# Queries and keys transposed and split in the projection stage and stored, in place of at each head pair of the attention

## The chip, the cores and the metric

One core of one Trainium2 chip runs the kernel. The metric is the device time of one execution in microseconds (us). The engines are TensorE (PE; its weight loads are shown as PEld), VectorE (DVE), ScalarE (ACT), GpSimd (POOL) and SyncE (SP). SP does no arithmetic in this kernel: it issues transfers. ACT and POOL issue transfers too, each in its own instruction stream. Every engine runs its instructions in the order in which they stand in its stream and waits at an instruction until what it needs is there.

## The reference

One inference step of a decoder layer for a prompt of 1024 rows (width 1024) and for 8 sample rows, which share all weights. Cut to what the change touches:

```python
h = rmsnorm(x) @ w_in                      # columns: q 512, k 512, v 512, gate logits 8, u 512, z 512
logf = log_sigmoid(h[..., O_F:O_U] + b_f)  # one forget gate per head and row
c = cumsum(logf, axis=1)
s = einsum('bqhd,bkhd->bhqk', q, k) * 64 ** -0.5      # 8 heads of 64
s = s + (c[query] - c[key])                            # causal mask behind it
att = einsum('bhqk,bkhd->bqhd', softmax(s), v)
```

Beside it the sample rows attend over 8192 cached keys each, in a paged cache (keys gathered, multiplied by the sample's query, summed over 64 columns). Then come a spatial gating of u and z, an output projection, a cross-attention into 256 memory rows and a gated MLP. The keys k and values v of the prompt are outputs too.

## The kernel before

**Three products for one.** All matrix products of the prompt run in a rounded 32-bit format with two parts: a number is split into a high part h (ACT copies it in the rounded format) and a low part l (DVE subtracts h from the number). A product is then three matmuls, h·h, h·l and l·h. The helper `split` (L232) does one split; weights arrive as `wr` and are split into `wh` (L235, ACT) and `wl` (L236, DVE).

**Stages of the prompt.** The projection, called p1, runs in column groups: Q, F (the 8 gate columns and u together, 520 columns), K, V, Z. A group loads four weight tiles of 128x1024 or 128x1040 and goes over eight row tiles of 128 rows, 24 matmuls each (F: 48 of 260 columns). `evac` (L467) then copies the bank with a row scale to a tile `t` and stores it: Q to the scratch `q_d`, K and V to the outputs. After p1 come the attentions of the first and of the second 512 rows, one behind the other; the first is mixed with the projection of the memory rows. Then come merge, cross-attention and MLP for the first and for the second half.

**Attention of one half** (`attention`, from L725). It goes over four head pairs, in each over blocks of queries and keys. The score product folds the split and the gates into the contraction: the operand `qq` has 64 rows of the query's high part over 64 rows of its low part, and a second piece with the high part and 4 gate rows; `ka` holds the key's high part twice, `kb` its low part with 4 gate rows. `load` (L730) loads a pair's queries and keys in rows, and the values. `setup` (L743) then transposes them on PE (L750 queries, L779 keys, four each), copies the high parts on ACT (L757, L784), copies these once more on POOL (L758, L785) and subtracts for the low parts on DVE (L774, L788). In the first half it also stores the split keys to `ks_d` from POOL (L791, L792), so that the second half loads those keys ready made. `LD` and `ST` are the places in the block loop at which the next pair's load and set-up are begun.

**The sample's work** is cut into steps that are mixed into the prompt's stages at a fixed pace (`PACE`, L76). In p1 a step gathers cached keys into `kv` (POOL), multiplies them by the sample's query `d` (DVE, L1444) and sums (DVE, L1448). That query is computed in group Q, stored by SP into `qs_d` (L465), and loaded from there spread over 128 partitions into `d` (SP, L1398).

**What sets the order.** The program is written as generators; a scheduler with a timeline model then puts each engine's instructions in order when the kernel is built. `behind(engine)` (L1369) and `issue_after` keep an instruction behind another one. The order is fixed before the run.

Of the kernel before, what the change touches and what calls it, by code (L numbers as in the profile page):

```python
# [60 lines left out]
LD = [(0, 1, 0), (0, 0, 0)]  # L61
ST = [(0, 1, 1), (0, 1, 1)]
# [5 lines left out]
NT = 7  # L68
# [3 lines left out]
SB = 2  # L72
# [6 lines left out]
def build(nc, tc, ctx, a, phases=None):  # L79
# [123 lines left out]
    q_d = dram.tile([T, AW], F32, tag="q_d", name="q_d")  # L203
# [6 lines left out]
    ks_d = dram.tile([NH, 64, 2, 512], F32, tag="ks_d", name="ks_d")  # L210
# [163 lines left out]
    def p1(early):  # L374
# [92 lines left out]
        def evac(ps, dst, sc, tt):  # L467
            t = T2()
            nc.scalar.activation(t, ps, AF.Copy, scale=sc[:, tt : tt + 1])
            nc.scalar.dma_start(dst[tt * P : (tt + 1) * P, :], t)  # L470
# [78 lines left out]
        for c0, dst in ((O_K, k_d), (O_V, v_d)):  # L549
            ws, sps = loaded(c0, 512, [(0, 512)])  # L550
            for tt in range(8):
                ps = BK()
                mm_chunk(tt, ws, ps, 0, 512)
                if tt == SD - 1:
# [15 lines left out]
                evac(ps, dst, rstd, tt)  # L570
# [155 lines left out]
    def attention(hf, queue, late=None, at=3):  # L726
# [3 lines left out]
        def load(hp):  # L730
            cs = slice(hp * P, (hp + 1) * P)
            qn = tpool.tile([P, 512], F32, tag="qn", bufs=1, name=nm("qn")).rearrange("p (i c) -> p i c", c=P)
            nc.sync.dma_start(qn, q_d[hf * 512 : (hf + 1) * 512, cs].rearrange("(i p) c -> p i c", p=P))
            if hf == 0:
                kvn = U([P, 2 * nk, P])
                kn, vn = kvn[:, :nk, :], kvn[:, nk:, :]
            else:
                kn, vn = T2().rearrange("p (i c) -> p i c", c=P), U([P, nk, P])
            nc.sync.dma_start(kn, k_d[hf * 512 : nk * P, cs].rearrange("(i p) c -> p i c", p=P))
            nc.sync.dma_start(vn, v_d[: nk * P, cs].rearrange("(i p) c -> p i c", p=P))  # L740
            return qn, kn, vn

        def setup(hp, qn, kn, vn):  # L743


            calm = lambda: tc.issue_after(lastexp[0]) if lastexp else nullcontext()
            with behind(ENG.PE):
                tr = BB() if hf else (MS, BB, BA)[SB]()
                for i in range(4):
                    nc.tensor.transpose(tr[:, i * P : (i + 1) * P], qn[:, i, :], ident)  # L750
            qab, ka, kb = [], [], []
            for j in range(2):
                h = hp * 2 + j
                rows = slice(64 * j, 64 * j + 64)
                qq = U([P, 2, 512], F32R)
                with calm():
                    nc.scalar.activation(qq[0:64, 0, :], tr[rows, :], AF.Copy)  # L757
                nc.gpsimd.tensor_copy(qq[0:64, 1, :], qq[0:64, 0, :].bitcast(F32))  # L758
                nc.gpsimd.dma_start(qq[64:68, 1, :], cq_d[h, :, hf * 512 : (hf + 1) * 512])
# [5 lines left out]
                else:  # L765
                    ka.append(U([P, nk * P], F32R))
                    kb.append(U([P, nk * P], F32R))
                    for r in range(2):
                        nc.sync.dma_start(ka[j][64 * r : 64 * r + 64, 0:512].bitcast(F32), ks_d[h, :, 0, :])
                    nc.sync.dma_start(kb[j][0:64, 0:512].bitcast(F32), ks_d[h, :, 1, :])  # L770
                nc.gpsimd.dma_start(kb[j][64:68, :], ck_d[h, :, : nk * P])
            for j, qq in enumerate(qab):
                rows = slice(64 * j, 64 * j + 64)
                nc.vector.tensor_tensor(qq[64:128, 0, :], tr[rows, :], qq[0:64, 0, :].bitcast(F32), op=ALU.subtract)  # L774
            yield
            with behind(ENG.PE):
                tr = BB() if hf else (MS, BB, BA)[SB]()
                for i in range(4):
                    nc.tensor.transpose(tr[:, i * P : (i + 1) * P], kn[:, i, :], ident)  # L779
# [110 lines left out]
        for _ in first:  # L890
            pass
# [1143 lines left out]
```

## Time and profile before

| | us |
|---|---|
| median of 3 runs | 1792.91 |
| lowest and highest run | 1789.93, 1795.33 |
| the profiled execution, first to last instruction | 1791.7 |
| PE busy | 1735.9 |
| DVE busy | 1399.9 |
| ACT busy | 733.5 |
| POOL busy | 488.3 |

The profile is one execution on its own; its span is what it has of a time of its own. A row of a time line reads: start, duration, engine (a q behind the name is its queue side, which issues transfers), line, operation, output <- inputs, shape, and in brackets the idle time ahead of it with what ended it. Names of tiles stand without their numbers there. PE's rows show 0.39 us for a matmul of 512 columns while the next begins 0.23 us later, since matmuls overlap. Group Q runs to 57.4 us, F from 62.2 to 111.8 us, Z ends at 239.95 us, the first scores of the attention start at 263.0 us and its last at 471.0 us.

### The profile page before, as it was taken

To read this page: it belongs to the slowest core of one execution; us is meant where nothing else is said; L and a number is where in the kernel's file an instruction comes from. 1 tells how busy PE (TensorE), PEld (TensorE's weight loads), DVE (VectorE), ACT (ScalarE), POOL (GpSimd) and SP (SyncE) were. 2 spreads that over 40 slices of the span, in tenths; PEclk is the share of its full clock that TensorE was granted. 3 is DMA by queue.
4 is the path that set the end of the run, shared out by engine and by line. 5 is a ranking of instruction groups with operands and counts; after the bars stand their busy time and mean duration, and the time that the engine had idled before them with its cause. 6 is when DMAs were issued, how large, how long until landed. Compare 5 with 4: busy or idle time off the path is not lost.

```text
span 1791.7 us, 25124 instructions
## 1 busy us (share of the span) xinstructions
PE 1735.9 (97%) x9653; PEld 1285.7 (72%) x9653; DVE 1399.9 (78%) x1733; ACT 733.5 (41%) x1374; POOL 488.3 (27%) x461
## 2 busy tenths in 40 slices
PE   8999999889999999999999999999999999999997
PEld 5787777655677666767777777766666778768875
DVE  4689658989788986989999999898885549855344
ACT  6332355566643635333333244335353233333232
POOL 1252234443222332333322223433322112102110
PEclk9999999999999999999999999999999999999999
DMA  8786798777697975779788788988879587568982
GB/s 291 297 304 226 294 334 319 259 264 244 254 403 279 363 299 224 282 285 345 290 301 313 291 317 311 376 306 346 320 280 350 214 306 249 191 260 297 359 310 80
DMA packets 157074, 521.06 MB, mean 291 GB/s; under 512 B 20874, under 2 KB 40842, under 8 KB 124186
## 3 DMA queue, kind: packets, MB, share of 16 engines
q0 software_dynamic: 57168, 341.14, 50.0%
q1 hardware_dynamic: 92874, 165.73, 26.5%
q10 hardware_dynamic: 6912, 12.59, 1.9%
q8 instruction: 76, 1.25, 0.3%
q14 instruction: 44, 0.36, 0.1%
HBM read 495.47 MB, written 23.93 MB: 290 GB/s over the span
## 4 chain that ended last, share of the span: by engine, by line
PE 53%; issue 9%; DMA 8%; DVE 6%; ACT 2%; POOL 2%; POOLq 0%; DVEq 0%; ACTq 0%; SPq 0%
DMA kv<-cache_v,io 6%; PE ba L272 6%; PE ba L274 6%; PE ba L273 6%; PE dv L1495 4%; PE bb L272 3%; PE bb L273 3%; PE bb L274 3%; PE ba L1063 1%; DVE s L1448 1%; PE ba L1064 1%; PE ba L1065 1%; PE dv L331 1%; DMA kv<-cache_k,io 1%; PE dv L1774 1%
## 5 line engine op out<-in xcount | busy, mean ns | idle before, releaser
L235 ACT ACTIVATE wh<-wr 128x1024 fp32r<-128x1024 f32 (+2 forms) x220 | 228.6, 1044 | 443.3 <-PE ba L273 142.3
L236 DVE TENSOR_TENSOR wl<-wr,wh 128x1024 fp32r<-128x1024 f32 (+2 forms) x220 | 262.7, 1200 | 165.1 <-PE ba L274 57.4
L1428 POOL DMA_INDIRECT kv<-cache_k,io x128 | 186.9, 1460 | 606.8 <-DVE s L1448 327.2
L1444 DVE TENSOR_TENSOR kv<-kv,d 128x1024 f32<-128x1024 f32 (+1 forms) x156 | 258.0, 1681 | 32.6 <-DMA kv<-cache_k,io 32.6
L1448 DVE TENSOR_REDUCE s<-kv 128x16 f32<-128x1024 f32 (+1 forms) x156 | 258.4, 1672 | 0.0
L1489 POOL DMA_INDIRECT kv<-cache_v,io x128 | 160.8, 1256 | 239.4 <-PE dv L1495 155.2
L272 PE MATMUL ba<-u,wh 128*128 128x512 f32 x528 | 209.3, 397 | 0.0
L274 PE MATMUL ba<-u,wl 128*128 128x512 f32 x528 | 209.0, 396 | 0.0
L273 PE MATMUL ba<-u,wh 128*128 128x512 f32 x528 | 208.5, 395 | 0.5 <-DVE u L239 0.5
L272 PE MATMUL ba<-wh,u 128*128 128x512 f32 (+1 forms) x495 | 186.1, 379 | 0.9 <-ACT u L235 0.9
L273 PE MATMUL ba<-wl,u 128*128 128x512 f32 (+1 forms) x495 | 185.1, 375 | 1.3 <-DVE wl L236 1.3
L274 PE MATMUL ba<-wh,u 128*128 128x512 f32 (+1 forms) x495 | 183.4, 375 | 0.0
L1495 PE MATMUL dv<-kv,s 128*32 128x512 f32 x1024 | 127.1, 598 | 1.6 <-DMA kv<-cache_v,io 1.6
L274 PEld LDWEIGHTS ba<-u,wl 128*128 128x128 f32 x528 | 99.2, 188 | 29.0 <-issue 6.5
L272 PEld LDWEIGHTS ba<-u,wh 128*128 128x128 f32 x528 | 99.3, 188 | 26.4 <-issue 4.8
L273 PEld LDWEIGHTS ba<-u,wh 128*128 128x128 f32 x528 | 99.2, 188 | 25.2 <-issue 2.3
L272 PEld LDWEIGHTS ba<-wh,u 128*128 128x128 f32 x495 | 93.0, 188 | 25.0 <-issue 6.5
L272 PE MATMUL bb<-u,wh 128*128 128x512 f32 x272 | 108.7, 400 | 0.0
L274 PE MATMUL bb<-u,wl 128*128 128x512 f32 x272 | 108.0, 398 | 0.0
L273 PE MATMUL bb<-u,wh 128*128 128x512 f32 x272 | 107.9, 397 | 0.0
L273 PEld LDWEIGHTS ba<-wl,u 128*128 128x128 f32 x495 | 93.0, 188 | 20.1 <-DVE wl L236 1.9
L274 PEld LDWEIGHTS ba<-wh,u 128*128 128x128 f32 x495 | 92.9, 188 | 19.5 <-issue 1.6
(454 smaller groups left out, 3310.6 us busy)
## 6 DMA issues: line engine op xcount, KB each, us to landing
wr<-w_up SPq DMA_DIRECT2D x88, 512.0 KB
kv<-w_up POOLq DMA_DIRECT2D x22, 1024.0 KB
wr<-w_down SPq DMA_DIRECT2D x40, 512.0 KB
kv<-w_down POOLq DMA_DIRECT2D x11, 1024.0 KB
wr<-w_in SPq DMA_DIRECT2D x16, 512.0 KB
wr<-w_o SPq DMA_DIRECT2D x16, 512.0 KB
wr<-w_cq SPq DMA_DIRECT2D x16, 512.0 KB
wr<-w_co SPq DMA_DIRECT2D x16, 512.0 KB
```

The lines of the kernel that those rows point to most:

```text
L235: nc.scalar.activation(h, src, AF.Copy)
L236: nc.vector.tensor_tensor(l, src, h.bitcast(F32), op=ALU.subtract)
L272: mmul(out, sh, mh, start=(i == 0), stop=False)
L273: mmul(out, sh, ml, start=False, stop=False)
L274: mmul(out, sl, mh, start=False, stop=(i == n - 1))
L331: mmul(ps[32 * j : 32 * j + 32, :w], xT[:, k, :] if nk == 8 else xT[:, k * 8 : k * 8 + 32], raw[:, q, j * w : (j + 1) * w], start=(k == 0) ...
L1063: mmul(pss[i], mh[k][:, tb], wh, start=(k == korder[0]), stop=False)
L1428: nc.gpsimd.indirect_dma_start(kv, None, a["cache_k"], off(kidx[:, b, ch : ch + 1]))
L1444: nc.vector.tensor_tensor(kvv[:, i : i + m, :], kvv[:, i : i + m, :], qb.unsqueeze(1).broadcast_to((P, m, 512)), op=ALU.mult)
L1448: nc.vector.tensor_reduce(s[:, ch * 4 + i : ch * 4 + i + m, :].rearrange("p k h -> p (k h)"), kvv[:, i : i + m, :].rearrange("p k (h d) -> ...
L1489: nc.gpsimd.indirect_dma_start(kv, None, a["cache_v"], off(kidx[:, b, ch : ch + 1]))
L1495: mmul(dv[32 * j : 32 * j + 32, :], s[:, ch * 4 : ch * 4 + 4, :].rearrange("p k h -> p (k h)"), kvv[:, j, :], start=(ch == 1), stop=(ch == ...
```

## The change

Queries and keys are now transposed and split behind the projection's tiles, by a new function `operand`: it transposes the evacuated tile (four transposes into one bank), splits the bank into h and l (128x512, two heads' 64 columns at once per transpose), and stores both into two new scratch tensors, `qt_d` and `kt_d`, which hold for each head 64 rows of high and 64 rows of low part over all 1024 positions. The two stores of h are issued by ACT, the two of l by SP, 64 rows of 4x128 columns each. An `operand` is not run with its tile but put on a list; `turn_over` runs the oldest one or two behind a later tile's matmuls. `q_d` and `ks_d` are gone, and K and V are still stored by `evac`.

In the attentions `load` now loads `qq`, `ka` and `kb` ready made, eleven loads per head pair from SP, and `setup` is gone with its transposes, copies, casts, subtractions, stores and yields. The second half loads a pair at place (0, 1, 0) of the block loop in place of (0, 0, 0). The pool of 512-column tiles has 8 buffers in place of 7, for which the one `qn` buffer is gone.

```diff
-LD = [(0, 1, 0), (0, 0, 0)]
-ST = [(0, 1, 1), (0, 1, 1)]
+LD = [(0, 1, 0), (0, 1, 0)]
-NT = 7
+NT = 8
-    q_d = dram.tile([T, AW], F32, tag="q_d", name="q_d")
+    qt_d = dram.tile([NH, P, T], F32, tag="qt_d", name="qt_d")
+    kt_d = dram.tile([NH, P, T], F32, tag="kt_d", name="kt_d")
-    ks_d = dram.tile([NH, 64, 2, 512], F32, tag="ks_d", name="ks_d")
...
+        def operand(t, dst, tt):
+
+            tr = BK()
+            for hp in range(4):
+                nc.tensor.transpose(tr[:, hp * P : (hp + 1) * P], t[:, hp * P : (hp + 1) * P], ident)
+            h, l = T2(512, F32R), T2(512, F32R)
+            split(tr, h, l)
+            d = dst.rearrange("(hp j) (r d) t -> j r d hp t", j=2, r=2)
+            for r, (q, src) in enumerate(((nc.scalar, h), (nc.sync, l))):
+                for j in range(2):
+                    q.dma_start(
+                        d[j, r][:, :, tt * P : (tt + 1) * P],
+                        src[64 * j : 64 * j + 64, :].bitcast(F32).rearrange("d (hp t) -> d hp t", t=P),
+                    )
+
+        def turn_over(n):
+            for _ in range(min(n, len(flat))):
+                flat.pop(0)()
...
                 mm_chunk(tt, ws, ps, 0, 512)
+                turn_over(2)
                 yield 5.2
-            evac(ps, q_d, rstd8, tt)
+            flat.append(partial(operand, evac(ps, None, rstd8, tt), qt_d, tt))
...
             mm_chunk(tt, ws, ps2[:, 0:260], 260, 260)
+            turn_over(1)
...
-                evac(ps, dst, rstd, tt)
+                t = evac(ps, dst, rstd, tt)
+                if c0 == O_K:
+                    flat.append(partial(operand, t, kt_d, tt))
...
+                nc.sync.dma_start(qq[:, 0, :].bitcast(F32), qt_d[h, :, s])
+                nc.sync.dma_start(qq[0:64, 1, :].bitcast(F32), qt_d[h, 0:64, s])
+                nc.gpsimd.dma_start(qq[64:68, 1, :], cq_d[h, :, s])
...
+                for r in range(2):
+                    nc.sync.dma_start(ka[j][64 * r : 64 * r + 64, :].bitcast(F32), kt_d[h, 0:64, : nk * P])
+                nc.sync.dma_start(kb[j][0:64, :].bitcast(F32), kt_d[h, 64:128, : nk * P])
```

**Where it moves instructions: DVE between Q and F.** Before, DVE's stream at the end of group Q reads as follows (`wl` are the low halves of F's weights, `kv` the sample's gathered keys, `d2_61` the sample's query, `s` the sums; the numbers tell tiles apart):

```order
L236 TENSOR_TENSOR wl_83_556<-wr_82_554,wh_84_557 128x1040
L236 TENSOR_TENSOR wl_86_566<-wr_85_564,wh_87_567 128x1040
L236 TENSOR_TENSOR wl_89_576<-wr_88_574,wh_90_577 128x1040
L236 TENSOR_TENSOR wl_92_586<-wr_91_584,wh_93_587 128x1040
L1444 TENSOR_TENSOR kv_63_348<-kv_63_348,d2_61_345 128x2048
L1444 TENSOR_TENSOR kv_64_388<-kv_64_388,d2_61_345 128x2048
L1444 TENSOR_TENSOR kv_70_453<-kv_70_453,d2_61_345 128x2048
L1444 TENSOR_TENSOR kv_73_485<-kv_73_485,d2_61_345 128x2048
```

The four low halves stand ahead of the first four multiplications. In the changed kernel the same place reads (lines are those of the changed file: L234 is the subtraction of `split`, L1419 the multiplication, L1423 the sum, L1383 a scan; `t` are low parts of query tiles):

```order
L234 TENSOR_TENSOR t_84_525<-ba_519,t_83_524 128x512
L1419 TENSOR_TENSOR kv_348<-kv_348,d_61_345 128x2048
L1419 TENSOR_TENSOR kv_388<-kv_388,d_61_345 128x2048
L1419 TENSOR_TENSOR kv_475<-kv_475,d_61_345 128x2048
L1419 TENSOR_TENSOR kv_532<-kv_532,d_61_345 128x2048
L1383 SCALAR_TENSOR_TENSOR d_157_1173<-rmask,d_157_1173 128x512
L1423 TENSOR_REDUCE s_347<-kv_348 128x32
L234 TENSOR_TENSOR t_90_569<-bb_563,t_89_568 128x512
L1423 TENSOR_REDUCE s_347<-kv_388 128x32
L234 TENSOR_TENSOR t_93_582<-ba_576,t_92_581 128x512
L234 TENSOR_TENSOR wl_639<-wr_637,wh_640 128x1040
```

The first low half of F's weights stands behind the four multiplications, a scan, two sums and two splits; the three others follow in the next six rows, with two sums and a scan between them.

**ACT in group Q.** In the changed kernel ACT's stream for the fourth to sixth evacuation reads (L467 is the evacuation, L233 the high part of a split, L484 a store into `qt_d`; `wh` is a weight's high half):

```order
L233 ACTIVATE wh_640<-wr_637 128x1040
L233 ACTIVATE t_71_454<-bb_449 128x512
L484 DMA qt_d<-t_71_454 64x4x128 x2
L233 ACTIVATE t_74_467<-ba_462 128x512
L484 DMA qt_d<-t_74_467 64x4x128 x2
L467 ACTIVATE t_77_479<-ba_424,rstd_123 128x512
L233 ACTIVATE t_80_511<-bb_506 128x512
L484 DMA qt_d<-t_80_511 64x4x128 x2
L233 ACTIVATE t_83_524<-ba_519 128x512
L484 DMA qt_d<-t_83_524 64x4x128 x2
```

Before, each evacuation was followed by one store into `q_d` (L470); now two copies and four stores of earlier tiles stand ahead of the fifth evacuation (`t_77`), and as many ahead of the sixth.

**SP ahead of the attention.** In the changed kernel SP's stream at the end of group Z reads (L636 stores the sample's gated row, L777, L778 load keys, L765, L766 queries):

```order
L636 DMA us_d<-t_115_677 8x512
L777 DMA u_2191<-kt_d 64x512 x2
L778 DMA u_2191<-kt_d 64x512
L765 DMA u_2196<-qt_d 128x512
L766 DMA u_2196<-qt_d 64x512
L777 DMA u_2200<-kt_d 64x512 x2
L778 DMA u_2200<-kt_d 64x512
```

Before, the store of `us_d` was followed by the next pair's queries (`qn`, L733), since the first pair's rows had been loaded ahead of it; now the first pair's keys stand behind that store.

More of the change, by code (lines that the diff above doesn't have):

```diff
@@ L71 @@
 LT = 3
-SB = 2
 KS = 2
@@ L731, in load @@
             cs = slice(hp * P, (hp + 1) * P)
[L732 to L739, printed above, removed]
[L740 to L750 removed]
+            vn = U([P, nk, P])
+            nc.sync.dma_start(vn, v_d[: nk * P, cs].rearrange("(i p) c -> p i c", p=P))
             qab, ka, kb = [], [], []
```

56 lines of the change are left out of this document (10 added, 46 removed).

## The prediction

> **What bounds the kernel now.** I read the page first, then a table of stretches, then the waits of PE, and last the time lines of the engines at the places where the change puts something.
>
> ```profile
> span 1791.7 us, 25124 instructions
> PE 1735.9 (97%) x9653; PEld 1285.7 (72%) x9653; DVE 1399.9 (78%) x1733; ACT 733.5 (41%) x1374; POOL 488.3 (27%) x461
> ```
>
> ```profile
> 40.00:60.00 20.00, 19.57 (x100) 14.73 (x98) 1.48 (x3) 7.41 (x13) 7.28 (x8) 1.00 0.98 395
> 60.00:80.00 20.00, 17.57 (x139) 15.39 (x134) 17.11 (x11) 11.78 (x17) 0.95 (x1) 1.00 0.62 221
> ```
>
> The second block is two rows of a table of 20 us stretches (columns: PE, PEld, DVE, ACT, POOL busy, granted clock, DMA share, GB/s). TensorE is the bound nearly everywhere. A change can therefore win in two ways only: by taking work off PE, or by taking away one of its few waits. It loses wherever it makes PE wait. The stretch from 60 us, between the groups Q and F of the projection, is one of the few in which PE already waits; before it the DMA is full (0.98). The table of stretches for the later stages:
>
> ```profile
> 112.00:166.00 54.00, 53.92 (x249) 39.27 (x242) 47.59 (x42) 18.89 (x26) 18.75 (x8) 1.00 0.68 227
> ...
> 208.00:240.00 32.00, 32.00 (x160) 21.52 (x159) 21.92 (x17) 10.94 (x19) 10.81 (x11) 1.00 0.95 361
> 240.00:350.00 110.00, 105.20 (x577) 80.42 (x576) 86.11 (x154) 63.12 (x136) 42.99 (x54) 0.98 0.84 306
> 350.00:460.00 110.00, 96.66 (x661) 65.86 (x659) 98.24 (x172) 72.07 (x162) 41.73 (x56) 0.95 0.78 258
> ```
>
> The last two rows are the two attentions. What PE waited for there (240 to 500 us) is a list of 16 rows, which add up to 19.2 us (line, releaser: total, times, longest):
>
> ```profile
> PE ba L807 <- ACT wr L817: 3.1, 7, 0.8
> ...
> PE bb L852 <- DVE u L774: 0.8, 1, 0.8
> ...
> PE ba L807 <- DVE u L774: 0.6, 1, 0.6
> ...
> PE ms L836 <- DVE u L841: 0.2, 1, 0.2
> ```
>
> Only two of these rows end at the set-up that goes (L774): 1.4 us.
>
> **Attention: what goes.** Each of the eight head pairs loses two groups of four transposes, four ACT copies (L757, L784), four subtractions on DVE (L774, L788) and four casts on POOL. Each row below has a twin of 8 more instructions with the other bank.
>
> ```profile
> L774 DVE TENSOR_TENSOR u<-bb,u 64x512 fp32r<-64x512 f32 x8 | 5.5, 689 | 0.2
> ...
> L757 ACT ACTIVATE u<-bb 64x512 fp32r<-64x512 f32 x8 | 4.7, 592 | 1.3 <-PE bb L750 1.2
> ...
> L784 ACT ACTIVATE u<-bb 64x512 fp32r<-64x512 f32 x8 | 4.7, 589 | 2.9 <-PE bb L779 2.5 <-PE ms L1481 0.3
> ```
>
> ```profile
> 239.72 0.39 PE L274 MATMUL bb<-wh,u 128*128 128x512 f32 x1
> 239.95 0.60 PE L750 MATMUL ba<-cp,qn 128*128 128x128 f32 x4
> 240.38 0.60 PE L779 MATMUL ba<-cp,u 128*128 128x128 f32 x4
> ```
>
> From the start of one group of transposes to the start of the next are 0.43 us, so 16 groups hold PE for 6.9 us. All of them come back behind the projection's tiles: on PE this is moved, not saved. DVE loses 32 × 0.689 = 22.0 us and ACT 32 × 0.59 = 18.9 us in attention; the projection gets 16 splits of 128x512, some 11 us on each. Both engines have room in attention. What a lighter ACT is worth there I can only bound: nothing, or all the waits, 19.2 us. ACT loses 18.9 of its 63.12 + 72.07 = 135.2 us, 14%; I take 14% of the other waits (17.8 us), 2.5 us, and the 1.4 us of L774 in full: **−4**, bounds 0 and −19. POOL's casts and stores were on nobody's path. The `yield`s of the set-up go too, so a few of the sample's steps move to later stages; they are the same work, priced at 0.
>
> The loads grow. A pair in the first attention read two inputs of 256 KB, v, and wrote 512 KB; it now reads 768 KB of queries and 768 KB of keys beside v, 0.5 MB more in all; in the second attention it is 1 MB more. That is 6 MB, 15 us at the 395 GB/s shown above. The idle DMA share is (0.16 + 0.22) × 110 = 42 us, so it fits, and the loads have a head pair's length of about 27 us (110 / 4). I price it at 0, up to +5 if some come late.
>
> **Between Q and F: what the new splits push aside.** This is the largest term.
>
> ```profile
> 53.19 1.24 DVE L236 TENSOR_TENSOR wl<-wr,wh 128x1040 fp32r<-128x1040 f32 x1 [7.73 <-PE ba L273]
> 62.79 3.74 DVE L236 TENSOR_TENSOR wl<-wr,wh 128x1040 fp32r<-128x1040 f32 x3 [8.36 <-ACT wh L235]
> 66.45 8.89 DVE L1444 TENSOR_TENSOR kv<-kv,d 128x2048 f32<-128x2048 f32 x4
> ...
> 75.39 1.21 DVE L1408 TENSOR_TENSOR_SCAN d<-rmask,d 128x512 f32<-128x512 f32 x1
> 76.52 8.84 DVE L1448 TENSOR_REDUCE s<-kv 128x32 f32<-128x2048 f32 x4
> ```
>
> ```profile
> 62.25 0.39 PE L272 MATMUL ba<-wh,u 128*128 128x260 f32 x1
> ...
> 66.58 0.39 PE L273 MATMUL ba<-wl,u 128*128 128x260 f32 x1 [0.35 <-DVE wl L236]
> ...
> 67.31 0.28 PE L272 MATMUL bb<-wh,u 128*128 128x260 f32 x1
> 67.42 0.28 PE L273 MATMUL bb<-wl,u 128*128 128x260 f32 x1
> ```
>
> ```profile
> 111.60 0.28 PE L274 MATMUL ba<-wh,u 128*128 128x260 f32 x1
> ```
>
> Today the four low halves of F's weights stand ahead of the sample's four multiplications, and PE runs through F from 62.25 to 111.8 us, waiting for these halves only briefly. In the changed order DVE comes to the four multiplications first; behind them stand a scan, the reductions, two new splits, and between these the four low halves. An engine takes its instructions in order, so F's weights now wait for whatever the multiplications wait for. That is `d`, the sample's query spread over the partitions:
>
> ```profile
> 35.20 2.84 SPq L465 DMA_DIRECT2D qs_d<-t  x1
> 61.45 0.34 SPq L1398 DMA_DIRECT2D d<-qs_d  x1
> ```
>
> ```profile
> SPq L1398 <- DMA qs_d<-t: 23.3, 1, 23.3
> ```
>
> SP stood 23.3 us until its little store had landed behind the weight loads, and could issue the load of `d` only at 61.45. The change leaves store and load where they were, with one new store between them, so `d` is there between 61.8 (the issue's end) and 66.45 (when the multiplications ran). From then on DVE needs, up to the last low half: multiplications 8.89, two scans 2.4, four reductions 8.84, two splits 1.4 (L774's 0.69 each), four low halves 5.0 (3.74 / 3 each): 26.5 us. From 66.45 that ends at 92.9, from 61.8 at 88.3; today it was 66.5. The DMA is at 0.98 until 60 us, so I take the late end.
>
> What PE does meanwhile: by the new order 54 of F's 384 matmuls stand ahead of the first that needs the last low half, today 19; 35 × 0.12 us (67.31 to 67.42 and on) = 4.2 us are thus done earlier. From 66.58 to 111.8 are 45.2 us, so F ends at 92.9 + 45.2 − 4.2 = 133.9, 22.1 us later. Eight of the sixteen groups of transposes, 3.5 us, lie inside this stall and are free, and attention loses them: net **+18.6**, lower bound +14.0 (from 88.3).
>
> Q itself also ends later, which this term covers:
>
> ```profile
> 59.37 0.69 ACT L469 ACTIVATE t<-bb,rstd 128x512 f32<-128x512 f32 x1 [11.02 <-DMA wr<-w_in]
> 61.26 0.33 ACTq L470 DMA_DIRECT2D q_d<-t  x1
> ```
>
> ACT stands for 11 us at a store's issue until weight loads have landed, around 61.3. Behind that row it now has the evacuation of the fifth tile, and PE has that tile's transposes ahead of the last tile. So the fifth tile is out of its bank only at about 62.2 (61.3, 0.69 and a little for the hand-over); with some 4 us for the sixth tile's evacuation behind two splits and their stores, and a last tile of 24 × 0.23 = 5.5 us (239.72 to 239.95 above), Q ends at about 72. F's first low half is not there before 66.45 + 8.89 + 1.2 + 2.2 + 0.7 + 2.2 + 0.7 + 1.25 = 83.6, so the lateness of Q costs nothing more; were the low halves early, it would cost 72 − 62 = 10 us.
>
> **A rule against my sum.** A row: the 16 KB store of `qs_d` was issued at 35.2 to 38.0 and held SP until 61.4. The Trainium skill, "DMA: Bandwidth & Descriptors", section "Latency and other measured facts", has an access to the outer memory at 2 us under high load and calls this most of the about 2 us that a DMA costs whatever its size. By that estimate the store would be down at about 40 and `d` a few us later, and the term above would be near 0. The row disagrees by a factor of ten; the same page, section "Issuing engines are not separate DMA queues", says why it can: transfers of all engines interleave on the same 16 DMA engines.
>
> **K, and the start of attention.** Behind each K tile come 4 transposes (moved), an ACT copy, a subtraction and four stores of 128 KB, two on ACT's queue and two on SP's. DVE is busy for 47.59 of the 54 us from 112 to 166; with 8 × 0.69 = 5.5 us more it is nearly full, and the low halves of V's weights queue behind these splits. Behind SP's new stores stand the loads of K's, V's and Z's weights: each now waits for a split. Lower bound 0, upper bound each tile's pair of 0.69 us (ACT's evacuation above, DVE's subtraction) in PE's way, 8 × 1.38 = 11; the trace shows PE 53.92 of 54 busy under much DVE load, which is nearer to nothing: **+2**.
>
> The first scores stand right behind Z in PE's new order. Their keys are loaded behind the `us_d` store on SP:
>
> ```profile
> 234.13 0.29 SPq L610 DMA_DIRECT2D us_d<-t  x1
> 240.58 0.38 SPq L733 DMA_DIRECT2D qn<-q_d  x1
> ```
>
> Six us before Z's end (239.95) SP comes free; some 1.2 MB of operands then take 3 us alone at 395 GB/s, but the DMA share there is 0.95 and the second row shows a free SP still held until 240.58. Between 0 and 8 us; **+3**.
>
> **The sum.** 1791.7 + 18.6 + 2 + 3 − 4 = 1811.3. The median of the three runs, 1792.91, is 1.2 us above the profiled span and within the runs' spread (1789.93 to 1795.33), so I forecast 1812.5, say **1812**. A measurement can tell about 0.3%, 5.4 us, from no change.
>
> **Rivals.**
> - *Faster: `d` comes early.* If the store of `qs_d` is not held up, the 26.5 us chain begins before Q's end; the point from which it decides is `d` landing at 66.5 − 26.5 = 40 us. Where ACT's stores are not held either, the Q to F term is then about 0 and PE's old waits there (62.25 to 66.58) hide the 3.5 us of transposes; attention gives 4 to 12 us, say 8: 1792.9 − 3.5 − 8 = 1781. Against it stands the row with 23.3 us. With large gains in attention counted in: 0.16. By the estimate from the Trainium skill's page the store would be down in time for this.
> - *No change.* The stall is at its lower bound (14.0) and attention gives back half or more of its 19.2 us of waits, with K and the start at 0: 1792.9 + 14 − 12 = 1795. For it: most of these waits end at ACT, which gets lighter. Against it: the waits end at exponentials and copies that stay. 0.12.
> - *Slower still: DVE and SP become the bound.* K at its upper 11, the start of attention at 8, loads late by 5, attention gives only 1.4: 1792.9 + 18.6 + 11 + 8 + 5 − 1.4 = 1834. For it: 112 to 166 leaves DVE hardly any room. 0.10.
> - *My forecast*: 0.62. Its own range goes from 1799 (stall 14.0, K and start 0, attention −8) to 1828 (stall 18.6, K 8, start 8, attention 0).
>
> The range takes in the bounds of these cases down to most of the faster one: 1785 to 1830. Chances: faster 0.16, within 0.3% 0.12, slower 0.72.
>
> **What would show it.** Right: in the time line of the changed kernel DVE's first `wl` for F starts past 78 us, the last ends at 88 to 93, PE waits there for DVE's `wl` for over 15 us in total, F ends at 130 to 137; SP again waits some 23 us for `qs_d`. PE's waits in attention shrink by a few us, and none there ends at DMA. Wrong: the multiplications start well before 60, or the `wl` come before them in time; or attention becomes shorter by over 15 us; or PE waits for DMA of `kt_d` or `qt_d` at every pair.

## The result and the profile after

The changed kernel takes 1849.68 us (median of 4 runs, 1845.47 to 1855.22) against 1793.11 us (four runs of the kernel before, one more than above); the ratio is 1.0305, with a 95% interval of 1.028 to 1.0329. It is slower by 56.6 us. Forecast were 1812 us and at most 1830: the direction held, the size did not.

The changed kernel's page begins so:

```profile
span 1849.2 us, 25145 instructions
PE 1758.2 (95%) x9653; PEld 1297.2 (70%) x9653; DVE 1386.8 (75%) x1703; ACT 727.5 (39%) x1360; POOL 449.2 (24%) x413
```

ACT, DVE and POOL have less to do, as the change says, and PE has as many instructions, but the span is 57.5 us longer. To see where, I paired each matmul of the prompt with the same one of the kernel before and took the difference of their starts; the median over a stretch of 40 us is the **delay** there (stretches by the time of the kernel before).

| stretch | group | delay, us |
|---|---|---|
| 80 to 120 | F | 20.5 |
| 200 to 240 | Z | 34.7 |
| 360 to 400 | second attention begins | 19.2 |
| 600 to 640 | after the attentions | 38.3 |
| 1040 to 1080 | first half's MLP | 36.1 |
| from 1760 | end | 58.1 |

So the change loses 20 us up to F and 14 in K, wins 15 in the first attention, loses 19 in the second and right behind it, and 20 more in the stages behind, whose own work it leaves as it was.

**Q and F.** DVE's time line in the changed kernel (start, duration, engine, line, operation, tiles):

```profile
63.94 8.89 DVE L1419 TENSOR_TENSOR kv<-kv,d 128x2048 f32<-128x2048 f32 x4
...
79.44 1.23 DVE L234 TENSOR_TENSOR wl<-wr,wh 128x1040 fp32r<-128x1040 f32 x1
...
87.25 2.39 DVE L234 TENSOR_TENSOR wl<-wr,wh 128x1040 fp32r<-128x1040 f32 x2
```

The first low half of F's weights comes at 79.4, behind the four multiplications, and the last ends at 89.6. PE's last row of F and the two rows of SP for `qs_d`:

```profile
132.13 0.28 PE L272 MATMUL bb<-wh,u 128*128 128x260 f32 x1
```

```profile
35.77 4.21 SPq L463 DMA_DIRECT2D qs_d<-t  x1
...
59.38 0.35 SPq L1373 DMA_DIRECT2D d<-qs_d  x1
```

All of that is near the forecast (88.3 to 92.9 for the last low half, 133.9 for the end of F, `d` issued around 61). But the wait that was to cause it, PE's for the low halves, hardly came: of PE's list for 55 to 135 us this is the row for them, beside 7.5 us for evacuations.

```profile
PE bb L271 <- DVE wl L234: 0.3, 1, 0.3
```

The last matmul of Q had started at 74.55 in place of 57.09, so 17.5 us were lost before F began: PE's long waits lie in Q. These are PE's rows, then ACT's:

```profile
60.33 0.66 PE L478 MATMUL bb<-cp,t 128*128 128x128 f32 x4 [1.86 <-ACT t L467]
66.55 1.11 PE L478 MATMUL ba<-cp,t 128*128 128x128 f32 x4 [5.56 <-ACT t L467]
67.31 0.78 PE L270 MATMUL ba<-wh,u 128*128 128x512 f32 x1
67.89 0.63 PE L271 MATMUL ba<-wl,u 128*128 128x512 f32 x1
68.31 0.63 PE L272 MATMUL ba<-wh,u 128*128 128x512 f32 x1
...
71.30 0.40 PE L270 MATMUL ba<-wh,u 128*128 128x512 f32 x1
71.54 0.39 PE L271 MATMUL ba<-wl,u 128*128 128x512 f32 x1
```

```profile
54.49 5.06 ACTq L484 DMA_DIRECT2D qt_d<-t  x2
59.59 0.69 ACT L467 ACTIVATE t<-ba,rstd 128x512 f32<-128x512 f32 x1 [7.72 <-DMA qt_d<-t]
```

PE waits for ACT's evacuations (L467). ACT stood 7.72 us: its queue side was held 5.06 us at two stores, and the releaser is a store's landing. Both end at about 59.6, so these rows alone do not tell which of the two decides. The two issues take only 0.58 us each; between them ACT stands at a counter. SP's and ACT's transfers report their landing through eight shared counters (semaphores 101 and 103 to 109), which the program deals out in turn, and a store waits until the transfer that had its counter before has landed. The second of these stores was issued at 58.96, its counter's last step had come at 58.94, and the transfer before on it was a weight load that SP issued at 33.43. The evacuated tile, its high part and its low part all come from the same eight buffers. A part's buffer is free only when its stores have landed; the evacuated tile's when it has been transposed (and, for a key tile, stored). The rows of PE show one thing more: after 5.56 us of idleness the matmuls start 0.43 us apart, not 0.23, until 71.3. The granted clock of that stretch (before the last two numbers of the row) says the same:

```profile
60.00:80.00 20.00, 13.31 (x72) 8.90 (x73) 17.36 (x12) 10.15 (x14) 1.75 (x2) 0.74 0.65 169
```

**K** shows the same wait in PE's list for 140 to 200 us, and on ACT:

```profile
PE ba L478 <- ACT t L467: 5.5, 2, 3.0
```

```profile
165.35 0.63 ACT L233 ACTIVATE t<-t 8x512 fp32r<-8x512 f32 x1 [9.56 <-DVE t L558]
...
171.07 0.60 ACT L233 ACTIVATE t<-bb 128x512 fp32r<-128x512 f32 x1 [1.80 <-DMA cq_d<-t]
```

The gate rows (8x512) use these buffers too; here they stand in ACT's stream ahead of the next evacuation and wait for DVE and then for stores of theirs.

**The attentions.** Rows of stretches from 400 to 440 us, before and after, each in its own kernel's time (last three numbers: granted clock, DMA share, GB/s):

```profile
400.00:440.00 40.00, 35.50 (x250) 23.76 (x249) 38.23 (x65) 25.03 (x50) 12.54 (x16) 1.00 0.82 271
```

```profile
400.00:440.00 40.00, 30.64 (x203) 20.77 (x202) 29.07 (x52) 20.87 (x46) 9.11 (x12) 0.91 0.99 272
```

The DMA, which had room, is full (from 320 to 480 us it moves 46.2 MB in place of 38.5), and PE is busy 30.6 us in place of 35.5. What it waits for is DVE, and DVE for the sample's gathered keys:

```profile
PE bb L823 <- DVE u L861: 6.8, 1, 6.8
```

```profile
436.71 0.69 DVE L1410 TENSOR_TENSOR kv<-kv,d 128x512 f32<-128x512 f32 x1 [8.76 <-DMA kv<-cache_k,io]
```

### The profile page after: what moved, and what is told of

It reads as the page before. It is cut to its first block, busy times and chain, and to the rows that moved or that the text cites. A ratio compares the mean times of both kernels' runs of the same rounds, so it can differ in the third digit from the quotient of the medians.

```text
span 1849.2 us, 25145 instructions
## 1 busy us (share of the span) xinstructions
PE 1758.2 (95%) x9653; PEld 1297.2 (70%) x9653; DVE 1386.8 (75%) x1703; ACT 727.5 (39%) x1360; POOL 449.2 (24%) x413
## 3 DMA queue, kind: packets, MB, share of 16 engines
q1 hardware_dynamic: 98634, 178.32, 28.7%
## 4 chain that ended last, share of the span: by engine, by line
PE 71%; DMA 12%; DVE 8%; issue 4%; ACT 3%; POOL 1%; ACTq 1%; SPq 0%; DVEq 0%; POOLq 0%
PE ba L270 9%; PE ba L271 9%; PE ba L272 9%; PE dv L1470 5%; PE bb L270 5%; PE bb L272 5%; PE bb L271 5%; DMA kv<-cache_k,io 2%; DMA wr<-w_in 2%; DVE s L1423 1%; DVE wl L234 1%; PE ba L1038 1%; DVE kv L1419 1%; PE ba L1040 1%; PE ba L1039 1%
## 5 line engine op out<-in xcount | busy, mean ns | idle before, releaser
L233 ACT ACTIVATE wh<-wr 128x1024 fp32r<-128x1024 f32 (+2 forms) x220 | 228.5, 1044 | 452.1 <-PE ba L271 138.1
L234 DVE TENSOR_TENSOR wl<-wr,wh 128x1024 fp32r<-128x1024 f32 (+2 forms) x220 | 262.7, 1201 | 151.1 <-PE ba L272 47.6
L1403 POOL DMA_INDIRECT kv<-cache_k,io x128 | 166.7, 1302 | 653.3 <-DVE s L1423 408.5
L1419 DVE TENSOR_TENSOR kv<-kv,d 128x1024 f32<-128x1024 f32 (+1 forms) x161 | 265.2, 1674 | 29.5 <-DMA kv<-cache_k,io 29.4
L1423 DVE TENSOR_REDUCE s<-kv 128x16 f32<-128x1024 f32 (+1 forms) x161 | 265.5, 1668 | 0.3
L1464 POOL DMA_INDIRECT kv<-cache_v,io x128 | 174.3, 1362 | 320.9 <-PE dv L1470 231.9
L271 PE MATMUL ba<-u,wh 128*128 128x512 f32 x544 | 216.5, 398 | 0.0
L270 PE MATMUL ba<-u,wh 128*128 128x512 f32 x544 | 216.4, 398 | 0.0
L272 PE MATMUL ba<-u,wl 128*128 128x512 f32 x544 | 215.9, 397 | 0.0
L270 PE MATMUL ba<-wh,u 128*128 128x512 f32 (+1 forms) x503 | 195.1, 388 | 10.1 <-DVE t L234 3.8
L271 PE MATMUL ba<-wl,u 128*128 128x512 f32 (+1 forms) x503 | 191.8, 382 | 0.0
L272 PE MATMUL ba<-wh,u 128*128 128x512 f32 (+1 forms) x503 | 189.4, 382 | 0.0
L271 PEld LDWEIGHTS ba<-u,wh 128*128 128x128 f32 x544 | 102.7, 189 | 32.4 <-issue 9.0
L270 PEld LDWEIGHTS ba<-u,wh 128*128 128x128 f32 x544 | 102.7, 189 | 24.3 <-issue 1.9
L270 PE MATMUL bb<-u,wh 128*128 128x512 f32 x256 | 101.9, 398 | 0.0
L271 PE MATMUL bb<-u,wh 128*128 128x512 f32 x256 | 101.3, 396 | 0.0
```

Of the source, the lines that this page charges most:

```text
L233: nc.scalar.activation(h, src, AF.Copy)
L234: nc.vector.tensor_tensor(l, src, h.bitcast(F32), op=ALU.subtract)
L270: mmul(out, sh, mh, start=(i == 0), stop=False)
L271: mmul(out, sh, ml, start=False, stop=False)
L272: mmul(out, sl, mh, start=False, stop=(i == n - 1))
L1403: nc.gpsimd.indirect_dma_start(kv, None, a["cache_k"], off(kidx[:, b, ch : ch + 1]))
```

## The experiments

All runs were timed beside runs of the kernel before on the same chip; the chip differs between groups of runs, so the ratios compare across the table better than the medians. Theories, as they came up: 1, order on DVE; 2, stores issued by ACT; 3, shared buffers; 4, the sample's steps; 5, DMA in the attentions. The delays are worked out as above, from one profiled execution each. In the four kernels whose projection is the same (changed kernel, steps_restored, second_copy_on_pool, pool_and_steps) F came out at 17.6 to 24.1 and Z at 31.8 to 39.6, so up to 8 us of a single delay can be chance.

| run | ratio (95% interval) | median | F | Z | 360 | 600 | end |
|---|---|---|---|---|---|---|---|
| changed kernel | 1.0305 (1.028 to 1.0329) | 1849.7 | 20.5 | 34.7 | 19.2 | 38.3 | 58.1 |
| all_on_sp | 1.0267 (1.0237 to 1.0297) | 1837.6 | 20.5 | 30.1 | 18.4 | 29.8 | 46.3 |
| multiplications_late | 1.0277 (1.0249 to 1.0304) | 1841.1 | 13.8 | 32.0 | 20.0 | 34.1 | 47.9 |
| late_and_sp | 1.0308 (1.0274 to 1.0341) | 1843.3 | 11.9 | 26.3 | 11.6 | 22.9 | 50.7 |
| keys_only | 1.0152 (1.0126 to 1.0177) | 1817.5 | -1.9 | 19.1 | 18.1 | 26.2 | 24.7 |
| own_buffers | 1.0278 (1.0243 to 1.0313) | 1844.4 | 18.4 | 24.1 | 8.2 | 24.6 | 53.1 |
| steps_restored | 1.0289 (1.0256 to 1.0322) | 1841.3 | 17.6 | 31.8 | 26.8 | 41.6 | 47.2 |
| own_and_steps | 1.0231 (1.0203 to 1.0259) | 1835.2 | 18.6 | 23.5 | 18.9 | 34.4 | 43.9 |
| queries_only | 1.015 (1.0125 to 1.0174) | 1818.9 | 19.3 | 19.4 | 13.8 | 18.6 | 25.3 |
| second_copy_on_pool | 1.0224 (1.0194 to 1.0254) | 1838.4 | 24.1 | 39.6 | 21.4 | 28.1 | 45.7 |
| pool_and_steps | 1.0186 (1.0156 to 1.0215) | 1831.5 | 19.9 | 32.7 | 26.7 | 35.8 | 45.2 |
| mixed_buffers | 1.015 (1.012 to 1.018) | 1823.2 | 8.7 | 13.7 | -0.5 | 13.4 | 26.1 |
| mixed_pool_steps | 1.011 (1.0076 to 1.0143) | 1818.9 | 10.0 | 15.1 | 14.3 | 18.7 | 29.1 |
| mixed_on_act | 1.0206 (1.0176 to 1.0237) | 1829.1 | 13.3 | 23.2 | 9.1 | 20.7 | 36.3 |
| queries_mixed | 1.0105 (1.0078 to 1.0133) | 1812.1 | 7.5 | 8.4 | 6.1 | 13.3 | 18.0 |
| before_no_steps | 1.0157 (1.0129 to 1.0184) | 1820.5 | -0.7 | -0.7 | -2.2 | 4.2 | 27.3 |

### Order on DVE or stores on ACT

The stores of the high part go to SP (all_on_sp); the sample's first four multiplications are kept back until F's weights are split (multiplications_late; `body` holds the multiplications and sums of one step); both (late_and_sp).

```diff
-            for r, (q, src) in enumerate(((nc.scalar, h), (nc.sync, l))):
+            for r, (q, src) in enumerate(((nc.sync, h), (nc.sync, l))):
```

```diff
+            if early_[0]:
+                put_off.append(body)
+            else:
+                body(behind(ENG.DVE))
...
         ws, sps = loaded(O_F, 520, [(8, 512), (0, 8)])
+        early_[0] = False
+        for body in put_off:
+            body(tc.issue_after(newest(ENG.DVE)))
```

> Changed kernel, but both high-part stores of a transposed tile are issued by SP instead of ACT. Theory 1 (the prediction's): between Q and F the low halves of F's weights are late because DVE has four multiplications ahead of them, so a shorter stop in Q is filled up by a longer wait in F; last low half still at 88 to 93 us, F still ends at 129 to 133; total gain over the changed kernel 0 to 8 us, mostly from group K: 1842 to 1850. Theory 2 (ACT's stores hold its evacuations and PE stops for those): the two stops of 2.0 and 5.7 us in Q and the 2.7 and 3.3 us in K go, with the slow matmuls behind them: 15 to 25 us faster than the changed kernel, 1825 to 1835.

> Changed kernel, but the sample's first four multiplications are put behind the low halves of F's weights in DVE's order. Theory 1 alone (order on DVE): last low half at 74 to 80 us in place of 89.6, F ends 8 to 12 us earlier, 1838 to 1842 in total. Theory 2 (ACT's stores in Q): F's waits for the low halves are only 4 us in the changed kernel, since PE itself is late out of Q; gain 0 to 5, 1845 to 1850.

> Both of the two edits: all stores from SP and the multiplications behind F's low halves. If the two causes cover each other (theory 1 with Q's own lateness hidden behind it), only this one takes the Q to F loss away: F ends at 113 to 118 us, gain over the changed kernel 18 to 28 us with K's part, 1822 to 1832, and more than the sum of the two single edits. If theory 2 alone holds, it equals the run with the stores on SP.

With the stores on SP, F is as late as ever (20.5), which is theory 1's mark, and what is won comes in K and later; the total, 1837.6, lies between what the two theories expected. With the multiplications late, F is 6.7 us earlier, a little less than theory 1 expected and more than theory 2 did (13.8 is 3.8 below the lowest of the four above); 4 us of it are lost again in K, and the total, 1841.1, is in theory 1's bracket. Both together bring F to 11.9, not to the level of the kernel before, and the total (1822 to 1832 was expected) is no better than the changed kernel. So neither order nor issue is the whole of it, and a delay of 23 us at 600 us still ended as 50: something else costs the end.

### One half of the change each

Only the keys, or only the queries, are transposed behind the projection; the other operand is loaded in rows and set up at each head pair as before (with its steps). The first diff is that of keys_only, the second that of queries_only, without the set-up that comes back. Both also load the second half's pairs at the old place (0, 0, 0) again, and keys_only has 7 buffers and the `qn` buffer again.

```diff
-            flat.append(partial(operand, evac(ps, None, rstd8, tt), qt_d, tt))
+            evac(ps, q_d, rstd8, tt)
```

```diff
-                if c0 == O_K:
-                    flat.append(partial(operand, t, kt_d, tt))
```

> Only the keys are transposed behind the projection and stored; queries as before (stored in rows, transposed at each head pair). Theories 1 and 2 both: the 20 us of Q to F are gone, K's 13 us stay, attention gains some 5: about 1800 to 1806 if the 20 us that the changed kernel loses after 480 us belong to the queries or to the missing set-up steps in attention, 1815 to 1825 if they are a consequence of K's or of stored keys.

> Only the queries are transposed behind the projection; keys as before. Theory 1 or 3: the delay of 20 us at F stays, K adds nothing, attention gives 3 to 8 back, and if the late loss comes with missing steps little is added: 1802 to 1815. If the late loss belongs to the stored queries: 1825 to 1840.

The queries alone carry Q and F (19.3), the keys alone K (from -1.9 to 19.1). Each then ends where it was at Z, within 6 us: the attentions give nothing back on balance. From 600 us to the end keys_only adds nothing (-1.5) and queries_only 6.7, against 19.8; both still have the set-up's steps. keys_only came out inside its second bracket, but not for the reason that went with it: the loss was there at Z. queries_only ended 4 us above its first bracket. Over the kernel before the two halves lose 26.8 and 29.0 us, which add up to nearly the whole 56.6 although both keep the steps; so the missing steps are not simply a share that comes on top.

### Buffers

The two parts of a transposed tile share one buffer of the larger pool, of which two are free during the projection (own_buffers); or only every second tile does, and the stores go to SP (mixed_buffers) or stay on ACT (mixed_on_act). The diff is that of the mixed runs; own_buffers has no condition.

```diff
-            h, l = T2(512, F32R), T2(512, F32R)
+            if tt % 2:
+                hl = U([P, 2, 512], F32R)
+                h, l = hl[:, 0, :], hl[:, 1, :]
+            else:
+                h, l = T2(512, F32R), T2(512, F32R)
```

> Changed kernel, but the high and low parts of a transposed tile lie in one buffer of the larger pool (two of its 18 are free in the projection) instead of two of the eight buffers that all evacuations share. Theory 3 (in both Q and K the evacuations wait for a shared buffer, which is held until a store has landed; the order on DVE only follows from that): the waits of PE for evacuations fall from 11 us in Q and 6 in K to under 5 together, F's low halves are there by 72, the delay against the kernel before at 200 us falls from 34.7 to 8 to 18 us; total 1820 to 1832. Theory 2 (the issue of the stores on ACT itself, 0.6 us each): no more than 6 us gained, 1843 or more.

> Changed kernel, but every second transposed tile takes a buffer of the larger pool for its two parts, and all of its stores are issued by SP. Theory 3 (shared buffers) with theory 2 (stores on ACT): DVE again has three of F's four low halves ahead of the multiplications, the delay at 200 us falls from 34.7 to 5 to 15 us; total 1815 to 1830 with the late loss as it is. If neither: 1840 or more.

> Mixed buffers as before, but the stores of the high part are issued by ACT again, as in the changed kernel. If the buffers decide: the delay at 200 us stays at 12 to 18 us, total 1820 to 1830. If ACT's issue of stores decides: delay at 200 us 25 to 35, total 1835 to 1848.

With two buffers for all tiles Q runs more freely (delay 8.1 from 40 to 80 us), but two are too few: in F, PE waits 7.3 us at once for the split into the next pair of parts, and from 80 us on most of the gain is gone. The delay at Z (24.1) is above the bracket of theory 3 and far below the changed kernel's, while the total is where theory 2 had it. With the mixture, DVE has three of the four low halves early again:

```profile
56.66 1.24 DVE L234 TENSOR_TENSOR wl<-wr,wh 128x1040 fp32r<-128x1040 f32 x1 [0.22 <-PE ba L271]
58.10 2.61 DVE L234 TENSOR_TENSOR wl<-wr,wh 128x1040 fp32r<-128x1040 f32 x2 [0.20 <-PE ba L271]
61.22 8.90 DVE L1423 TENSOR_TENSOR kv<-kv,d 128x2048 f32<-128x2048 f32 x4 [0.51 <-DMA d<-qs_d]
```

The delay at Z falls from 34.7 to 13.7, and about 7 of that are the 64 transposes that PE now does here. With the same buffers and the stores on ACT it is 23.2, from this:

```profile
48.57 8.65 ACTq L488 DMA_DIRECT2D qt_d<-u  x2
57.27 0.69 ACT L467 ACTIVATE t<-ba,rstd 128x512 f32<-128x512 f32 x1 [9.61 <-DMA wr<-w_in]
```

ACT stands at its stores behind weight loads, as the prediction said, with evacuations behind it. The issues take 0.62 and 0.58 us; from 49.2 to 56.6 the second store waits for its counter, on which a weight load landed at 56.62. So buffers take 11.5 us of the projection's loss (34.7 to 23.2) and the issue by ACT 9.5 (to 13.7); taken the other way round, the issue alone is worth 4.6 (all_on_sp, 30.1) and the buffers behind it 16.4. The two cover each other: at the end of Q (54 to 58 us) the delay is 17.5 us in the changed kernel, 12.6 in all_on_sp, 15.9 in mixed_on_act and 3.5 with both. mixed_on_act lies between its two brackets at Z and inside the first in total. The buffers also decide the order: the scheduler put three low halves ahead of the multiplications once the parts did not queue for buffers.

### The sample's steps

The set-up of a head pair gave five unit steps to the pace of the sample's work. They are given again without any work (steps_restored, and own_and_steps with own buffers); and, the other way round, they are taken from the kernel before, whose set-up is left as it is (before_no_steps).

```diff
                             nxt = load(hp + 1)
+                        if hp < 3 and (blk, j, ii) >= (0, 1, 1):
+                            yield 1
```

```diff
                         if nxt:
                             next(nxt, None)
-                            yield 1
```

> Changed kernel, but the five unit steps per head pair that the set-up gave to the sample's pace in the attentions are given again (empty). Theory 4 (the 30 us that all kernels without the set-up lose after 480 us come from sample steps that were shifted to other places): the delay grows by 0 to 8 us after 480 us in place of 33, total 1818 to 1832. If the late loss has another cause: 1845 to 1853.

> Both: own buffers for the transposed parts, and the unit steps given again. If theories 3 and 4 hold, what is left of the projection's loss is 8 to 18 us, attention gives 10 to 16 back and the rest is as before: 1785 to 1805, level with the kernel before. If theory 4 fails: 1820 to 1832.

> The kernel before, with the set-up's work unchanged, but without the unit steps that it gave to the sample's pace. Theory 4 (steps that fall elsewhere): the delay against the kernel before is below zero in the attentions (0 to -10 us) and rises by 8 to 20 us after 600 us; total 1795 to 1805. If the late loss belongs to the change's own instructions: within 4 us of the kernel before.

before_no_steps is the plainest of all the runs. Nothing of the change is in it but the missing steps, and it takes 1820.5 us: 29 us more than the kernel before, and more than I had expected of it (1795 to 1805). Its delay is below zero in the second attention (-2.2), 4.2 at 600 us, and 27.3 at the end. PE's waits from 1000 us on, in this run and in the kernel before, the longest rows:

```profile
PE dv L1494 <- DMA kv<-cache_v,io: 4.5, 1, 4.5
PE ba L272 <- ACT u L235: 4.1, 2, 2.4
PE ba L280 <- DVE u L1014: 2.3, 1, 2.3
```

```profile
PE bb L280 <- ACT u L238: 1.7, 1, 1.7
PE ba L1188 <- ACT t L1175: 1.4, 2, 0.8
```

The sample's work was paced so that its gathers, multiplications and matmuls fell between the prompt's; with 30 unit steps less in the attentions (two or three of the sample's steps by `PACE`), every later step falls elsewhere. PE's order shows it. For each of the sample's matmuls into `dv`, count the prompt's matmuls and transposes that PE had begun before it. For those that ran from 600 to 1550 us in the kernel before, the count is higher by 26 to 204 in each of the nine kernels that lack the steps (the changed one, seven with it changed, and before_no_steps). In each of the seven that have them it is at most 13 higher and 31 lower.

In the nine the delay grows by 12.7 to 28.5 us from 600 us to the end, in the seven by -1.5 to 10.4. The clean part of this lies behind 1400 us: 9.7 to 12.8 us in the nine, 0 to 1.4 in the seven. Between 600 and 1400 the two groups overlap. One thing before_no_steps does not separate: the unit steps also set how the projection of the memory rows is mixed into the first attention, so the prompt's own order changes there too.

What the missing steps win in the attentions takes part of the loss away again: over the kernel before on the same chip, giving them back gained 5, 9 and 7 us in the three pairs of runs (56.6 to 51.4, 54.5 to 45.3, 43.1 to 36.2). The intervals of each pair overlap; it is the three together that point one way. Both totals were above the forecasts (1841.3 for 1818 to 1832, 1835.2 for 1785 to 1805).

### DMA in the attentions

The second copies of the high parts are made by POOL, as before, in place of a second load: 5 MB less.

```diff
-                nc.sync.dma_start(qq[0:64, 1, :].bitcast(F32), qt_d[h, 0:64, s])
+                nc.gpsimd.tensor_copy(qq[0:64, 1, :], qq[0:64, 0, :].bitcast(F32))
...
-                for r in range(2):
-                    nc.sync.dma_start(ka[j][64 * r : 64 * r + 64, :].bitcast(F32), kt_d[h, 0:64, : nk * P])
+                nc.sync.dma_start(ka[j][0:64, :].bitcast(F32), kt_d[h, 0:64, : nk * P])
+                nc.gpsimd.tensor_copy(ka[j][64:128, :], ka[j][0:64, :].bitcast(F32))
```

> Changed kernel, but the second copies of the high parts in the attentions (64 rows of each query and key operand) are made by POOL instead of loaded a second time: 5 MB fewer loads. Theory 5 (from 320 to 480 us the DMA is full, 46 MB in place of 39, and the sample's gathers and the operands come late): the rise of the delay by 16 us between 360 and 560 us shrinks to 0 to 6, total 1834 to 1842. If the DMA does not matter: 1846 or more; if POOL's copies come in the way of the sample's gathers, which POOL issues: above 1850.

> Second copies on POOL and the sample's unit steps given again. Theories 4 and 5 together: the projection's loss of 32 us stays, the attentions lose nothing on the kernel before and give 5 to 10 back, later stages add no more than 5: 1815 to 1828, below each of the two single edits. If the late loss comes from elsewhere: 1835 or more.

From 360 to 600 us the delay grows by 6.7 in place of 19.1; with the steps given, by 9.1 in place of 14.8. The ratio falls from 1.0305 to 1.0224, with intervals apart. Over the kernel before that is 13.5 us less (56.6 to 43.1), and with the steps given 15.2 (51.4 to 36.2). Theory 5 holds, though it does not take all of the rise. In steps_restored, where the second loads are still there, PE's list for 380 to 480 us shows the loads themselves:

```profile
PE ba L796 <- DMA u<-cq_d: 5.9, 1, 5.9
PE ba L794 <- DMA u<-kt_d: 3.4, 1, 3.4
...
PE ba L796 <- DMA u<-kt_d: 1.7, 1, 1.7
```

pool_and_steps missed its bracket (1815 to 1828) by 3.5 us.

### All three, and the best of the halves

> All three edits (mixed buffers with SP's stores, second copies on POOL, steps given again). If theories 3, 4 and 5 name the three places at which the change lost, this takes most of it back: 1788 to 1806, level with the kernel before. If a loss of another kind is left: 1815 or more.

> Queries only, with mixed buffers and SP's stores; keys as in the kernel before. If the queries' loss was the stop between Q and F (delay 19 us at 200): it falls to 3 to 10, and the total to 1798 to 1808. If the queries lose in attention or later: 1812 or more.

All three mends bring the change from 56.6 us above the kernel before to 24 (1818.9 against 1795.3 on its chip), not level with it; that is the second bracket, a loss of another kind is left. 15 us of delay are left at Z, the attentions give none of it back (18.7 at 600 us), and 10 come after. Queries alone with the mixed buffers are the nearest, at 1.0105, just inside their second bracket: F's part went as expected (19.4 to 8.4 at Z), but attention adds 5 and the later stages 5. No version found beats the kernel before.

## Why the prediction was wrong

Put as delays, with the transposes counted where they run (3.5 us behind K, 6.9 us gone from the attentions), the forecast was 22.1 us at F, +5.5 in K, +3 at the start of attention, -10.9 in the attentions and 0 behind them. Measured were 20.5, +14.2, -1.2, +4.8 and +19.8.

- **Q to F: right in size, but by luck.** Last low half, end of F and the load of `d` came as worked out. But PE was to wait over 15 us for the low halves and waited 0.3: it came out of Q 17.5 us late, by waits for evacuations and splits. That lateness, priced at 10 and called covered, was most of the delay, and with the multiplications moved away F gained only 6.7 us. (ACT's old wait of 11 us, taken to end around 61.3, ends at 59.4 by its own row.) Under it lay a cause that I had not named: three tiles where there was one in the same eight buffers, with ACT's stores waiting behind weight loads beside it. The store of `qs_d` was in the way as forecast (issued at 35.8, `d` loaded from 59.4); the wait of 2 us by the Trainium skill's page did not come.
- **K: +5.5 forecast, +14.2 measured.** I took the row of PE's full stretch as the nearer bound. The wait was not the ACT and DVE time per tile that I had bounded at 11 but, again, buffers held by stores, with the gate rows in between: with own buffers K adds 5.7 us (18.4 to 24.1), with the mixed ones 5.0.
- **The start of attention: +3 forecast, about nothing measured** (34.7 at Z, 33.5 in the next stretch).
- **Attention: -10.9 forecast, +4.8 measured.** The first attention won 15 us up to 360, but most of that hangs on the missing steps: from Z to 360 the three kernels without them win 15.5 to 18.2 us, and the same three with them 4.6 to 6.0. From 360 to 600 it lost 19. The extra loads, priced at 0 to +5, filled the DMA (0.82 to 0.99) and held up the sample's gathers and the operands; 5 of the 6 MB were worth 13.5 to 15.2 us.
- **The steps that failed.** The largest by delay: "The `yield`s of the set-up go too, so a few of the sample's steps move to later stages; they are the same work, priced at 0." The work is the same, but its place is not: 29 us on the kernel before alone. In the changed kernel the stages behind the attentions lose 19.8 us without the steps and 5.6 with them; as the first attention wins by their absence, the net is only 5 to 9. The second: the loads, "I price it at 0, up to +5 if some come late", at 13.5 to 15.2. The third: the new splits were priced by the time of ACT and DVE, and the buffers that hold their parts until the stores have landed were left out; mixed buffers with SP's stores take 28.7 us off the total (56.6 to 27.9). These sizes do not add up to the whole, since the causes cover each other.
- **The rivals.** Slower still (1834) had the right sign of the K and DMA terms and still fell short, as it lacked the steps and the buffers. The faster one did not come: `d` was loaded from 59.4 in place of 61.45.

**What stays open.** Which of the sample's later steps meets which piece of the prompt was not followed row by row; that the missing steps cost the late loss is shown, the single collisions are not. Nor was it found why the mended kernels get nothing back in the attentions, where seven us of transposes less should show: with all three mends 24 us are left. The later place of the second half's loads, (0, 1, 0) for (0, 0, 0), was never tried alone, and neither were counters that loads and stores do not share.

## What to carry to other kernels

Where background work is paced by a count of the foreground's steps, a step is part of the tuning even if it does nothing: keep the count when work is taken out, or pace it anew, and try the old kernel with the new count to see what that alone costs. When work is moved behind a producer, count the buffers that it holds until its stores have landed, and ask what else waits for the same pool; an engine that both evacuates banks and issues stores can pass the wait of a store on to the matmuls, so ask what a long issue waits for. An operand made ready in memory is paid for in loads: look at the DMA's share in the stretch where it is read, not at its mean.

## What the runs showed of the hardware

A wait of PE can cost more than its length. After 5.56 us without work the next matmuls began 0.43 us apart in place of 0.23 for 4 us (67.3 to 71.3), and the granted clock was 0.50 from 66.5 to 71.3; over the whole run it was 0.979 against 0.993. Splitting the 58 us by PE's start-to-start times against the median of the same shape in the kernel before, some 42 are gaps of over 0.25 us and some 16 are slower matmuls and smaller gaps. The Trainium skill says much the same in "TensorE: Matmul & The Clock Gate", section "Part 1: The HAM clock gate": after a window of about 3.4 us without work the clock is halved, until about as long a time of work has passed. The waits in Q agree with that: one of 3.0 us (ending at 52.65) was followed by matmuls 0.33 and then about 0.24 apart. A wait in F does not: it was 2.30 us (ending at 84.74), and the matmuls of 260 columns behind it began 0.22 us apart in place of 0.12, at a granted clock of 0.62 from 84 to 88. So the length of a single wait does not decide it here.

Where a store is issued matters here though all queues share the DMA. The Trainium skill, "DMA: Bandwidth & Descriptors", section "Issuing engines are not separate DMA queues", says that issuing on several engines saves only the sequencer's time, usually a small part. The issues here agree: about 0.6 us each. With the mixed buffers the two stores of each high part from ACT in place of SP cost 9.5 us at Z all the same (4.6 with the shared buffers), since ACT also stood there for the counters: the row of 8.65 us for two stores holds 7.4 us of waiting for a weight load to land.
